# A second weight slab loaded in the retention, and a norm scale in operations of four blocks (Hyena and RetNet block, one core)

## The chip, the cores and the metric

One core of one Trainium2 chip runs the kernel. The metric is the device time of one execution in microseconds (us): the median of several executions, lowest and highest beside it. One further execution was recorded by the hardware profiler, and all rows of the trace come from that one. The engines are PE (TensorE: matrix products; its weight loads are a line of their own, PEld), DVE (VectorE), ACT (ScalarE), POOL (GpSimd, hardly used here) and SP (SyncE, which issues nearly all DMAs). Each engine takes its instructions in the order in which they stand in its queue.

## The reference

One layer works on 1024 tokens (and 256 of context) of width 1024. A norm and modulation feed one input projection; half of the columns go through a gated long convolution, half through a retention of 8 heads, in chunks of 128 tokens and in both directions; one output projection takes both halves; a second norm and an MLP with squared ReLU follow.

```python
x = x + gate1 * (concat(hyena, retention) @ w_out)
h = _modulate(_rmsnorm(x), shift2, scale2)
x = x + gate2 * (jnp.square(relu(h @ w_mlp1)) @ w_mlp2)
```

## The kernel before

**Numbers.** Each matrix product is made of three (`mm3`, lines 183 to 185): both operands are split into a high part in a shorter format and a low rest, and high x high, high x low and low x high are summed. So each operand is cast on ACT (the high part) and subtracted on DVE (the low part). Nothing is multiplied before both have been done for it.

**Weight slabs.** `slab` (from line 194) loads a slab of weights in two halves through one raw buffer (`wraw`, DMA on line 205), casts each half on ACT (206) and subtracts on DVE (207). The results go to two alternating buffers, unless the caller names a place. `prefetch()` loads the next slab in a list: the slabs of the input projection, the last four being g0, g1, q0, q1, and then o0 and o1, the first two column halves of the output weights for the convolution's part. It runs under `urgent()`, a raised priority. A scheduler sets each engine's order from priorities and dependencies; so a row in a queue need not stand where its line stands in the program.

**The entry of the retention.** The queries are computed last in the input projection: for each of two head halves `hh` and two groups, products (`pq`), a rotation on DVE (lines 569, 573, 579) and a store (1008). After each `hh` a `prefetch()` runs: o0 after the first, o1 after the second. Both take the buffers of a q slab that the products have read. Then `split_mix` reads the convolution's result, already in DRAM, in eight pieces of 128x512 through a ring of four slots (`mraw`, line 1055), and casts and subtracts each (1057, 1058) into `mx`: for k of 0 to 3 and token half 0 or 1. `out_conv(d)` multiplies all of `mx` by a 128-column block of slab o0 (d of 0 to 3) or o1 (d of 4 to 7) into `poh` (psum) and adds it to the stream XN (1069). The retention's loop over `(hh, g, j)` runs one chunk of tokens each time (`retention`; transposes `pqd`, scores `psc`, output `po`) and an `out_conv` after every second chunk. At `(0, 0, 2)` it loads slab o2, at `(1, 0, 0)` the raw data of the last slab, o3; both serve the retention's part of the output projection, at the end.

**The entry of the MLP.** `out_ret(q)` computes that part (`por`) for token half q, adds it to XN (1254), sums the squares and gives `rB2`, 1/rms of each of the 512 tokens, in all partitions. `right_factors(q, ...)` then makes the right operands of the MLP's first product. XN lies in two tiles of four 128-row blocks, XN0 and XN1. `modulated(k)` scales a block by `rB2` on DVE (1287) and applies scale and shift on ACT (1288); it runs for the blocks in the order 0, 4, 1, 5, 2, 6, 3, 7. The first product uses a scheme of seven block products in place of eight (`ORDER = (1, 5, 2, 6, 3, 7, 4)`), for which `part` (1186, 1187) splits the quarters y11, y12 (of XN0), y21, y22 (of XN1) and sums of them: b11, t1 (from y12 - y11, line 1296), b21, t2 (from u, line 1302), and b22, t3, t4. The step f=0 of the product runs for the first 256 columns, then the next 256; from f=1 on all 512 go at once.

The steps with odd f take their raw weights through CH, which has XN1's place (`w1_load`, line 1209), and WH, in XN0's place, takes the second product's weights (load 1399, sums 1401 to 1404, store 1405 to `s_d`). So both loads wait until the last part has been read from XN.

Of the kernel before, what the change touches and what calls it, by code (L numbers as in the profile page):

```python
# [12 lines left out]
AF = mybir.ActivationFunctionType  # L13
ALU = mybir.AluOpType
# [126 lines left out]
def tile_hymba_block(ctx: ExitStack, tc: tile.TileContext, I: dict, out: bass.AP, dbg=None, stop=99):  # L141
# [79 lines left out]
    def prefetch(n=1):  # L221
        for _ in range(n):
            if nxt[0] < len(order):
                key, src = order[nxt[0]]
                with urgent() if nxt[0] > 1 else ExitStack():
                    slabs[key] = slab(src, f"{key[0]}{key[1]}")
                nxt[0] += 1
# [770 lines left out]
    for hh in range(2):  # L998
        for g, ps in token_major(("q", hh), f"pq{hh}"):
            with urgent():  # L1000
                for m in range(2):
                    n0 = 4 * g + 2 * m

                    q2 = scp.tile([P, 2, 4, 2, HD], F32, tag="sc", bufs=3, name=f"q2{hh}{n0}")
                    qr = scp.tile([P, 2, 256], F32, tag="bfs", bufs=2, name=f"qr{hh}{n0}")
                    rope(qr, ps[:, 2 * m:2 * m + 2], ropes, n0, scp, f"q{hh}",
                         twice=q2.rearrange("p j h r d -> p (j h) r d"), tag="bfs", bufs=2)
                    SP.dma_start(q2_d[hh][n0:n0 + 2].rearrange("j p n -> p j n"),
                                 q2.rearrange("p j h r d -> p j (h r d)"))
            if hh == 0 and g == 0:  # L1010
                dbg("mod2", mod2)
        prefetch()
    cpool("cvp")
    cpool("vtp")
    cpool("scp")
# [122 lines left out]
    for hh in range(2):  # L1138
        for g in range(2):
            ctr = ctrs[:, g]  # L1140
            gss = rtp.tile([P, 4, 4], F32, tag="gss", bufs=2, name=f"gss{hh}{g}")
            for j in range(4):
                retention(hh, 4 * g + j, ctr, gss)
                if hh == 0 and g == 0 and j == 0:
                    for d in range(KC):
                        SP.dma_start(xn[d], I["xT"][d * P:(d + 1) * P])
                if j == 1 and pending:
                    group_norm(*pending)
                if j == 1:
                    SP.dma_start(sg.rearrange("p n d -> p (n d)"), sg_d[hh][g])  # L1150
                if j % 2:
                    out_conv(4 * hh + 2 * g + j // 2)
                if (hh, g, j) == (0, 0, 2):
                    wo = [slab(I["w_out"][2], "o2", o2)]
                if (hh, g, j) == (1, 0, 0):

                    o3r = wpool.tile([P, 4, 512], F32, tag="wh", bufs=2, name="o3r")
                    SP.dma_start(o3r, I["w_out"][3])
            pending = hh, g, sg, ctr, gss
# [116 lines left out]
    def right_factors(q, rB2, some):  # L1276
# [4 lines left out]
        def part(key, src):  # L1281
            hi, lo = B[key]
            split(hi[:, :, qs], lo[:, :, qs], src)

        def modulated(k, eng):
            y = xn[k][:, 512 * q:512 * q + 512]
            eng.tensor_tensor(y, y, rB2, op=ALU.mult)
            A.activation(y, y, AF.Identity, bias=B2[:, k:k + 1], scale=A2[:, k:k + 1])

        with urgent():  # L1290
            if 0 in some:
                for k in range(4):
                    modulated(k, V)
                    modulated(4 + k, V)
                part("b11", y11)
                V.tensor_tensor(y11, y12, y11, op=ALU.subtract)
                part("t1", y11)
                part("b21", y21)
                for h in range(2):
                    ks = slice(2 * h, 2 * h + 2)  # L1300
# [290 lines left out]
```

## Time and profile before

| | us |
|---|---|
| median of 3 runs | 1394.17 |
| lowest, highest | 1394.14, 1402.15 |
| profiled execution | 1399.48 |
| its span (first to last instruction) | 1397.7 |

The mean granted clock of TensorE in the profiled execution is 0.973 of full speed. The profiled execution lies within the three runs. Times in the rows are counted from the start of its span. In a row of the timeline the first number is the start, the second the time from there to the end of the last of a group, "x4" the number of instructions, and what stands in square brackets is how long the engine had stood idle and what ended it. Busy times of PE are modelled, and successive matmuls overlap; the distance of two starts is the price of one.

### The profile page before, as it was taken

The page shows a single profiled execution, that of the slowest core. Times are in us where ns is not written, and L with a number is a line of the kernel's source. Part 1 is how long each engine was busy: PE and PEld are TensorE (multiplying, and loading weights), DVE is VectorE, ACT ScalarE, POOL GpSimd, SP SyncE. Part 2 cuts the span into 40 slices and gives each one's busy share as a digit, 9 for nine tenths or more (in the row PEclk, how much of TensorE's full clock was granted, in tenths as well). Part 3 has the DMA queues.
Part 4 walks back from the last instruction along what each step waited for, and adds up shares of the span by engine and source line. Part 5 has one row for each costly group of instructions (what it writes and reads, how often), then busy time and mean ns, then how long its engine had stood idle before and what let it go on. Part 6 is the DMA issues. An engine that isn't in the chain of part 4 may idle for free.

```text
span 1397.7 us, 19336 instructions
## 1 busy us (share of the span) xinstructions
PE 1314.7 (94%) x7002; PEld 1108.2 (79%) x7002; DVE 974.2 (70%) x1733; ACT 533.3 (38%) x912; POOL 19.5 (1%) x24
## 2 busy tenths in 40 slices
PE   6899999999999999799996999999998999999997
PEld 1478888887788999688776788788786888888896
DVE  5889686447888775557887887887765865554563
ACT  6854422222132121223355444344444743444420
POOL 0130000000000000000000000000000000000000
PEclk9799999999999999899997999999999999999999
DMA  9445766363536644865320788899735996666621
GB/s 374 168 159 174 231 193 187 101 194 126 170 119 220 187 166 159 291 199 157 107 102 20 237 309 290 313 341 316 258 133 182 334 312 208 197 191 191 194 90 61
DMA packets 139567, 278.14 MB, mean 199 GB/s; under 512 B 14672, under 2 KB 47056, under 8 KB 137040
## 3 DMA queue, kind: packets, MB, share of 16 engines
q1 hardware_dynamic: 137744, 272.19, 58.7%
q0 software_dynamic: 1152, 4.19, 0.7%
q8 instruction: 55, 0.90, 0.3%
q10 hardware_dynamic: 576, 0.52, 0.1%
q14 instruction: 40, 0.33, 0.1%
HBM read 193.75 MB, written 83.10 MB: 198 GB/s over the span
## 4 chain that ended last, share of the span: by engine, by line
PE 70%; DVE 12%; DMA 11%; ACT 4%; issue 2%; SPq 1%; POOL 0%; DVEq 0%; ACTq 0%; POOLq 0%
PE px L183 6%; PE px L184 6%; PE px L185 6%; PE py L183 5%; PE py L184 5%; PE py L185 4%; PE pw L183 4%; PE pw L185 4%; PE pw L184 3%; DMA WH<-in_w_mlp 3%; PE pga L397 1%; DMA s_d<-WH 1%; DMA dft_f_k<-in_dft_f 1%; PE poh L183 1%; PE poh L184 1%
## 5 line engine op out<-in xcount | busy, mean ns | idle before, releaser
L1187 DVE TENSOR_TENSOR mt<-tr,mt 128x512 fp32r<-128x512 f32 x112 | 76.7, 688 | 97.0 <-ACT mt L1186 96.7
L1186 ACT CAST mt<-tr 128x512 fp32r<-128x512 f32 x112 | 69.5, 621 | 121.6 <-PE py L185 65.4
L183 PE MATMUL px<-mt,mw 128*128 128x512 f32 (+1 forms) x320 | 112.4, 352 | 2.7 <-ACT mw L1186 2.1
L184 PE MATMUL px<-mt,mw 128*128 128x512 f32 (+1 forms) x320 | 112.7, 353 | 1.2 <-DVE mt L1187 1.2
L185 PE MATMUL px<-mt,mw 128*128 128x512 f32 (+1 forms) x320 | 111.7, 350 | 0.0
L1187 DVE TENSOR_TENSOR mw<-wr,mw 128x512 fp32r<-128x512 f32 x112 | 76.6, 686 | 8.0 <-ACT mw L1186 7.5
L183 PE MATMUL py<-mt,mw 128*128 128x512 f32 x192 | 74.7, 389 | 0.0
L184 PE MATMUL py<-mt,mw 128*128 128x512 f32 x192 | 74.7, 389 | 0.0
L185 PE MATMUL py<-mt,mw 128*128 128x512 f32 x192 | 74.7, 389 | 0.0
L1186 ACT CAST mw<-wr 128x512 fp32r<-128x512 f32 x112 | 69.0, 617 | 12.2 <-DMA wr<-in_w_mlp 5.9
L183 PEld LDWEIGHTS px<-mt,mw 128*128 128x128 f32 x320 | 61.0, 191 | 11.3 <-ACT mw L1186 2.6
L184 PEld LDWEIGHTS px<-mt,mw 128*128 128x128 f32 x320 | 61.2, 191 | 9.4 <-DVE mt L1187 1.5
L185 PEld LDWEIGHTS px<-mt,mw 128*128 128x128 f32 x320 | 61.1, 191 | 8.3 <-DVE mw L1187 0.3
L183 PE MATMUL px<-hxh,wh_x 128*128 128x512 f32 x128 | 52.2, 407 | 0.0
L184 PE MATMUL px<-hxl,wh_x 128*128 128x512 f32 x128 | 51.9, 405 | 0.0
L185 PE MATMUL px<-hxh,wl_x 128*128 128x512 f32 x128 | 51.5, 402 | 0.0
L712 DVE SCALAR_TENSOR_TENSOR adac<-adaw,cs,adac 128x512 f32<-128x512 f32 x56 | 42.9, 766 | 11.7 <-DMA adaw<-in_w_ada 11.0
L185 PEld LDWEIGHTS py<-mt,mw 128*128 128x128 f32 x192 | 36.0, 188 | 7.5
L183 PEld LDWEIGHTS py<-mt,mw 128*128 128x128 f32 x192 | 36.0, 188 | 7.5
L184 PEld LDWEIGHTS py<-mt,mw 128*128 128x128 f32 x192 | 36.0, 188 | 7.4
L185 PE MATMUL pk<-wh_k,hxl 128*128 128x256 f32 x128 | 38.5, 301 | 3.3 <-DVE hxl L438 3.3
L183 PE MATMUL pk<-wh_k,hxh 128*128 128x256 f32 x128 | 40.1, 313 | 0.4 <-ACT hxh L434 0.4
(500 smaller groups left out, 3819.9 us busy)
## 6 DMA issues: line engine op xcount, KB each, us to landing
tr<-t_d SPq DMA_DIRECT2D x112, 256.0 KB, 4.0
adaw<-in_w_ada SPq DMA_DIRECT2D x64, 256.0 KB, 3.6
WH<-in_w_mlp SPq DMA_DIRECT2D x16, 1024.0 KB, 6.8
s_d<-WH SPq DMA_DIRECT2D x16, 1024.0 KB, 5.3
wr<-s_d SPq DMA_DIRECT2D x64, 256.0 KB, 4.0
wr<-in_w_mlp SPq DMA_DIRECT2D x48, 256.0 KB, 4.1
t_d<-c SPq DMA_DIRECT2D x40, 256.0 KB, 4.3
t_d<-CH SPq DMA_DIRECT2D x40, 256.0 KB, 5.0
```

Of the source, the lines that this page charges most:

```text
L183: PE.matmul(o, lhsT=lh, rhs=rh, start=first, stop=False, **kw)
L184: PE.matmul(o, lhsT=lh, rhs=rl, start=False, stop=False, **kw)
L185: PE.matmul(o, lhsT=ll, rhs=rh, start=False, stop=last, **kw)
L397: PE.matmul(pga[h][0:4, n, :], lhsT=cv[:, k, :], rhs=w_[:, n * 512:(n + 1) * 512], start=(k == 0), stop=(k == KC - 1 and i == 1))
L712: V.scalar_tensor_tensor(ac, wa, cs[:, k, 0:1], ac, op0=ALU.mult, op1=ALU.add)
L1186: A.copy(hi, src)
L1187: V.tensor_tensor(lo, src, hi.bitcast(F32), op=ALU.subtract)
```

## The change

The first part: `prefetch()` after the queries runs for `hh == 0` alone, so slab o1 is asked for inside the retention's loop, at `(0, 0, 1)`, and slab o2 one chunk later, at `(0, 0, 3)`. A debugging line that issues nothing goes. The second part: the norm scale of four blocks is one DVE operation of 128x4x512 with `rB2` repeated, followed by the four ACT operations of these blocks; blocks 0 to 3 come ahead of b11 and t1, blocks 4 to 7 behind them.

```diff
--- before.py
+++ after.py
@@ -1007,9 +1007,8 @@
                          twice=q2.rearrange("p j h r d -> p (j h) r d"), tag="bfs", bufs=2)
                     SP.dma_start(q2_d[hh][n0:n0 + 2].rearrange("j p n -> p j n"),
                                  q2.rearrange("p j h r d -> p j (h r d)"))
-            if hh == 0 and g == 0:
-                dbg("mod2", mod2)
-        prefetch()
+        if hh == 0:
+            prefetch()
     cpool("cvp")
     cpool("vtp")
     cpool("scp")
@@ -1150,7 +1149,9 @@
                     SP.dma_start(sg.rearrange("p n d -> p (n d)"), sg_d[hh][g])
                 if j % 2:
                     out_conv(4 * hh + 2 * g + j // 2)
-                if (hh, g, j) == (0, 0, 2):
+                if (hh, g, j) == (0, 0, 1):
+                    prefetch()
+                if (hh, g, j) == (0, 0, 3):
                     wo = [slab(I["w_out"][2], "o2", o2)]
                 if (hh, g, j) == (1, 0, 0):
 
@@ -1282,19 +1283,21 @@
             hi, lo = B[key]
             split(hi[:, :, qs], lo[:, :, qs], src)
 
-        def modulated(k, eng):
-            y = xn[k][:, 512 * q:512 * q + 512]
-            eng.tensor_tensor(y, y, rB2, op=ALU.mult)
-            A.activation(y, y, AF.Identity, bias=B2[:, k:k + 1], scale=A2[:, k:k + 1])
+        def modulated(i):
+
+            y = XH[i][:, :, 512 * q:512 * q + 512]
+            V.tensor_tensor(y, y, bc(rB2, 1, [P, 4, 512]), op=ALU.mult)
+            for k in range(4 * i, 4 * i + 4):
+                o = xn[k][:, 512 * q:512 * q + 512]
+                A.activation(o, o, AF.Identity, bias=B2[:, k:k + 1], scale=A2[:, k:k + 1])
 
         with urgent():
             if 0 in some:
-                for k in range(4):
-                    modulated(k, V)
-                    modulated(4 + k, V)
+                modulated(0)
                 part("b11", y11)
                 V.tensor_tensor(y11, y12, y11, op=ALU.subtract)
                 part("t1", y11)
+                modulated(1)
                 part("b21", y21)
                 for h in range(2):
                     ks = slice(2 * h, 2 * h + 2)
```

Line numbers below 1009 are the same in both; the ones behind are lower by one up to line 1150, and then higher by one (1254 becomes 1255), from the norm scale's lines on by two or three.

On SP, at the end of the queries: `wr_o11` is the raw second half of slab o1, `q214` and `q216` the last two groups of queries, `mraw` the mix ring. Before:

```order
L1036 DMA tabq_5409<-tab_d_1411 128x2048
L205 DMA wr_o11_5379<-in_w_out 128x1024
L1008 DMA q2_d1_4396<-q214_5357 128x2x512
L1055 DMA mraw_5417<-mix_d0_2896 128x512 x2
L1008 DMA q2_d1_4396<-q216_5365 128x2x512
L1055 DMA mraw_5417<-mix_d1_2897 128x512 x2
L1055 DMA mraw_5417<-mix_d2_2898 128x512 x2
L1079 DMA q2l0_0_5445<-q2_d0_4395 128x512
```

and after the change:

```order
L1035 DMA tabq_5399<-tab_d_1411 128x2048
L1054 DMA mraw_5407<-mix_d0_2896 128x512
L1008 DMA q2_d1_4396<-q214_5357 128x2x512
L1054 DMA mraw_5407<-mix_d0_2896 128x512
L1054 DMA mraw_5407<-mix_d1_2897 128x512
L205 DMA wr_o11_5552<-in_w_out 128x1024
L1008 DMA q2_d1_4396<-q216_5365 128x2x512
L1054 DMA mraw_5407<-mix_d1_2897 128x512
L1054 DMA mraw_5407<-mix_d2_2898 128x512 x2
L1054 DMA mraw_5407<-mix_d3_2899 128x512
L1078 DMA q2l0_0_5435<-q2_d0_4395 128x512
L1054 DMA mraw_5407<-mix_d3_2899 128x512
```

The second half's load stands behind three mix pieces now; the first half's, three rows above the first row shown, has not moved.

On ACT, at the same place: `wh_o1` is the high part of slab o1, `mx00` and `mx10` the high parts of the mix for the two token halves. Before:

```order
L206 CAST wh_o1_5373<-wr_o10_5375 128x1024
L206 CAST wh_o1_5373<-wr_o11_5379 128x1024
L1057 CAST mx00_5411<-mraw_5417 128x512
L1057 CAST mx10_5413<-mraw_5417 128x512
L1057 CAST mx00_5411<-mraw_5417 128x512
L1057 CAST mx10_5413<-mraw_5417 128x512
L1057 CAST mx00_5411<-mraw_5417 128x512
L1057 CAST mx10_5413<-mraw_5417 128x512
L1057 CAST mx00_5411<-mraw_5417 128x512
```

and after:

```order
L206 CAST wh_o1_5546<-wr_o10_5548 128x1024
L1056 CAST mx00_5401<-mraw_5407 128x512
L1056 CAST mx10_5403<-mraw_5407 128x512
L1056 CAST mx00_5401<-mraw_5407 128x512
L206 CAST wh_o1_5546<-wr_o11_5552 128x1024
L1056 CAST mx10_5403<-mraw_5407 128x512
L1056 CAST mx00_5401<-mraw_5407 128x512
L1056 CAST mx10_5403<-mraw_5407 128x512
L1056 CAST mx00_5401<-mraw_5407 128x512
L1056 CAST mx10_5403<-mraw_5407 128x512
```

The cast of the second half stands behind three of the eight mix casts, ahead of five. On DVE its subtraction likewise stands behind three of the eight of the mix, and that of the first half, `wl_o1`, which stood ahead of q214, stands ahead of q216. On PE 28 poh matmuls stood ahead of the one that takes the low part of the last mix piece for d = 0; 36 stand ahead of it now.

On DVE, at the MLP's entry for the second token half, from the norm scale on. The last two multiplications of eight and what follows, before:

```order
L1287 TENSOR_TENSOR XN0_5392<-XN0_5392,rB21_6804 128x512
L1287 TENSOR_TENSOR XN1_5393<-XN1_5393,rB21_6804 128x512
L1187 TENSOR_TENSOR b11l_6600<-XN0_5392,b11h_6599 128x4x256
L1187 TENSOR_TENSOR b21l_6604<-XN1_5393,b21h_6603 128x4x256
L1296 TENSOR_TENSOR XN0_5392<-XN0_5392 128x4x256
L1187 TENSOR_TENSOR b22l_6807<-XN1_5393,b22h_6806 128x4x256
L1302 TENSOR_TENSOR u210_6841<-XN1_5393,XN0_5392 128x512
L1187 TENSOR_TENSOR t1l_6602<-XN0_5392,t1h_6601 128x4x256
L1187 TENSOR_TENSOR t2l_6606<-u210_6841,t2h_6605 128x2x256
L1305 TENSOR_TENSOR XN1_5393<-XN1_5393,u210_6841 128x2x256
L1302 TENSOR_TENSOR u211_6846<-XN1_5393,XN0_5392 128x512
L1306 TENSOR_TENSOR XN0_5392<-XN1_5393,XN0_5392 128x4x256
```

and from the first multiplication on, after:

```order
L1289 TENSOR_TENSOR XN0_5382<-XN0_5382,rB21_6798 128x4x512
L1289 TENSOR_TENSOR XN1_5383<-XN1_5383,rB21_6798 128x4x512
L1188 TENSOR_TENSOR b11l_6600<-XN0_5382,b11h_6599 128x4x256
L1298 TENSOR_TENSOR XN0_5382<-XN0_5382 128x4x256
L1305 TENSOR_TENSOR u210_6829<-XN1_5383,XN0_5382 128x512
L1305 TENSOR_TENSOR u211_6834<-XN1_5383,XN0_5382 128x512
L1188 TENSOR_TENSOR b21l_6604<-XN1_5383,b21h_6603 128x4x256
L1188 TENSOR_TENSOR t1l_6602<-XN0_5382,t1h_6601 128x4x256
L1188 TENSOR_TENSOR t2l_6606<-u210_6829,t2h_6605 128x2x256
L1308 TENSOR_TENSOR XN1_5383<-XN1_5383,u210_6829 128x2x256
L1188 TENSOR_TENSOR t2l_6606<-u211_6834,t2h_6605 128x2x256
L1308 TENSOR_TENSOR XN1_5383<-XN1_5383,u211_6834 128x2x256
```

Two rows of four blocks take the place of eight, and the subtraction of b21 and that of t1 stand behind both u.

On ACT, the same place. Before, from the sixth of the eight operations on:

```order
L1288 ACTIVATE XN1_5393<-XN1_5393,mod2_1379,A2_1380 128x512
L1288 ACTIVATE XN0_5392<-XN0_5392,mod2_1379,A2_1380 128x512
L1288 ACTIVATE XN1_5393<-XN1_5393,mod2_1379,A2_1380 128x512
L1186 CAST b11h_6599<-XN0_5392 128x4x256
L1186 CAST b21h_6603<-XN1_5393 128x4x256
L1186 CAST b22h_6806<-XN1_5393 128x4x256
L1374 COPY c1_0_6996<-pw1_0_0_6997 128x256
L1186 CAST t1h_6601<-XN0_5392 128x4x256
L1357 COPY s1_1_0_256_7106<-pw1_0_256_7093 128x256
```

and after, all eight:

```order
L1377 COPY c1_0_6984<-pw1_0_0_6985 128x256
L1292 ACTIVATE XN0_5382<-XN0_5382,mod2_1379,A2_1380 128x512 x4
L1292 ACTIVATE XN1_5383<-XN1_5383,mod2_1379,A2_1380 128x512
L1187 CAST b11h_6599<-XN0_5382 128x4x256
L1292 ACTIVATE XN1_5383<-XN1_5383,mod2_1379,A2_1380 128x512 x3
L1187 CAST b21h_6603<-XN1_5383 128x4x256
L1187 CAST t1h_6601<-XN0_5382 128x4x256
L1187 CAST t2h_6605<-u210_6829 128x2x256
L1187 CAST t2h_6605<-u211_6834 128x2x256
```

The cast of b11 stands behind five of the eight operations in place of all. On SP the two loads of CH stand ahead of the first load of WH now, where a load of WH stood first, and on PE the first products of the step f=1 stand ahead of the last products (t3, t4) of f=0's second token half.

## Rows read from the trace of the kernel before

**Rows 1.** The page's first part: busy time, share of span, instructions

```profile
PE 1314.7 (94%) x7002; PEld 1108.2 (79%) x7002; DVE 974.2 (70%) x1733; ACT 533.3 (38%) x912; POOL 19.5 (1%) x24
```

**Rows 2.** Waits of PE: who waited for whom; us, times, longest one

```profile
PE poh L183 <- ACT mx L1057: 9.1, 1, 9.1
...
PE pw L183 <- ACT b11h L1186: 6.5, 1, 6.5
```

**Rows 3.** Windows: us, busy us (count) of PE, PEld, DVE, ACT, POOL; PEclk, DMA share, GB/s

```profile
566.00:579.47 13.47, 5.44 (x12) 3.66 (x13) 9.78 (x15) 3.93 (x7) 0.00 (x0) 0.62 0.77 253
...
753.94:763.70 9.76, 8.45 (x36) 7.86 (x36) 9.29 (x10) 4.05 (x6) 0.00 (x0) 0.50 0.01 2
...
763.70:773.90 10.20, 7.12 (x50) 6.07 (x49) 6.04 (x9) 5.37 (x7) 0.00 (x0) 0.99 0.51 181
...
773.90:777.40 3.50, 1.73 (x6) 1.16 (x7) 3.48 (x5) 2.45 (x5) 0.00 (x0) 1.00 0.92 306
...
777.43:780.80 3.37, 3.37 (x10) 2.61 (x8) 2.53 (x5) 1.41 (x4) 0.00 (x0) 0.51 0.88 260
...
780.80:800.00 19.20, 19.20 (x86) 15.88 (x85) 18.32 (x30) 9.06 (x15) 0.00 (x0) 1.00 0.54 199
...
940.00:980.00 40.00, 38.34 (x170) 31.45 (x169) 32.29 (x50) 17.67 (x28) 0.00 (x0) 1.00 0.91 321
```

**Rows 4.** Timeline of PE: start, us, instruction, [idle before <-releaser]

```profile
574.03 0.79 PE L183 MATMUL poh<-mx,wh_o 128*128 128x512 f32 x1 [9.06 <-ACT mx L1057]
...
574.76 0.79 PE L184 MATMUL poh<-mx,wh_o 128*128 128x512 f32 x1
...
584.97 0.40 PE L184 MATMUL poh<-mx,wh_o 128*128 128x512 f32 x1
```

**Rows 5.** Timelines of SP, ACT and DVE at the retention's entry

```profile
559.19 0.46 SPq L1036 DMA_DIRECT2D tabq<-tab_d  x1
...
565.01 1.04 ACT L206 CAST wh_o<-wr_o 128x1024 fp32r<-128x1024 f32 x1 [15.32 <-PE pq L185]
...
570.83 1.16 DVE L579 TENSOR_TENSOR q<-qr,rpq 128x1024 f32<-128x1024 f32 x1
...
571.98 1.22 DVE L207 TENSOR_TENSOR wl_o<-wr_o,wh_o 128x1024 fp32r<-128x1024 f32 x1
...
583.35 0.69 DVE L1058 TENSOR_TENSOR mx<-mraw,mx 128x512 fp32r<-128x512 f32 x1 [0.36 <-ACT mx L1057]
```

**Rows 6.** DMA issues from 566 and from 581: count, KB each, us to landing

```profile
mraw<-mix_d SPq DMA_DIRECT2D x8, 256.0 KB, 4.3
...
wr_o<-in_w_out SPq DMA_DIRECT2D x1, 512.0 KB, 3.4
...
XN<-in_xT SPq DMA_DIRECT2D x8, 512.0 KB, 7.9
```

**Rows 7.** Timelines of DVE, ACT and SP at the MLP's entry, second half

```profile
746.48 4.90 DVE L1287 TENSOR_TENSOR XN<-XN,rB 128x512 f32<-128x512 f32 x8 [0.83 <-ACT rB L1271]
...
767.67 1.21 DVE L1187 TENSOR_TENSOR t4l<-XN,t4h 128x1024 fp32r<-128x1024 f32 x1
...
747.21 5.75 ACT L1288 ACTIVATE XN<-XN,mod,A 128x512 f32<-128x512 f32 x8 [0.76 <-DVE XN L1287]
...
752.86 1.03 ACT L1186 CAST b11h<-XN 128x1024 fp32r<-128x1024 f32 x1
...
774.19 0.62 ACT L1186 CAST w<-CH 128x512 fp32r<-128x512 f32 x1
...
768.91 0.82 SPq L1209 DMA_DIRECT2D CH<-in_w_mlp  x2
```

**Rows 8.** Tile XN from 746 to 760: ns min/median/max, first and last start

```profile
L1287 DVE TENSOR_TENSOR XN<-XN,rB x8: 681/683/691, 746.5 to 750.7; 128x512 f32<-128x512 f32 x8
...
L1296 DVE TENSOR_TENSOR XN<-XN x1: 1218/1218/1218, 756.2 to 756.2; 128x1024 f32<-128x1024 f32 x1
```

**Rows 9.** Waits of DVE from 781 to 1080: us, times, longest one

```profile
DVE WH L1401 <- DMA WH<-in_w_mlp: 15.4, 10, 3.2
```


## The prediction

> **What bounds the kernel now.** I read the page first: PE is busy 94% of the span [rows 1], so only the places where PE stands still, or runs at the lower clock, can be won. The next view is PE's own waits: the long ones that the change can touch are 9.1 us ahead of poh (the first multiplication of the convolution's output), and 6.5 us ahead of pw behind b11h (the MLP's second token half) [rows 2]. The third is the windows, which give PE's busy time and clock for each stretch around these places [rows 3]. [...] Then 763.7 to 777.4 holds (10.20 - 7.12) + (3.50 - 1.73) = 4.85 us of idle PE at full clock, and 777.4 to 780.8 is low again. From 780.8 on PE has no gaps for long: 86 matmuls in 19.2 us, 0.223 us each, my price of a matmul of 512 columns at full clock. Last I read the timelines of ACT, DVE, SP and PE at both places [rows 4, 5], and the same for the MLP's entry.
>
> **Term A, the retention's entry.** Only the second half of slab o1 moves; its first half has its place still between the queries, by the order of SP. What falls away ahead of poh is one DVE subtraction (L207 at 571.98, 1.22 us) and one ACT cast of 1.04 us; the mix loads, which stood on SP behind that half's DMA and its wait for a free buffer, now come right behind tabq's load at 559.19 [rows 5]. A mix load lands in 4.3 us [rows 6], so the first piece is there when ACT is free: cast of the first half until 565.01 + 1.04 = 566.05, cast of mix 0.62, first poh at 566.7 instead of 574.03. It is one or two matmuls only, since the next needs the low part, which stands on DVE behind the last query operation. That one ends at 571.98 as before (the first half's subtraction has moved from ahead of the one query to ahead of the other, and the sum is the same), and 0.69 us later, at 572.7, PE can go on; before, the same matmul began at 574.76 [rows 4].
>
> How much of these 2.1 us stays is decided by the last of the eight mix pieces, since the ring has four slots. The second half's load is issued when DVE has freed its buffer, which is right ahead of the last query operation at 570.83 [rows 5], lands 3.4 us later [rows 6] at 574.3 to 574.9, and takes 1.04 us on ACT and 1.22 on DVE ahead of the fourth mix piece, whose slot the eighth waits for: 577.9, plus 4.3 of landing, 0.62 and 0.69, is 583.5; before, that subtraction ended at 584.04 [rows 5]. So the last pieces come hardly sooner, and PE gains by having done more ahead of them. Of PE's order I take the matmul with the low part of poh0's last piece (584.97, [rows 4]): 28 poh matmuls stand ahead of it before, 36 now. It begins some 0.2 us sooner with 8 x 0.223 = 1.8 us more done: A = -2.0. Bounds: -4.9, if PE also came to its full clock earlier (2.1, and 12 matmuls at 5.44 / 12 = 0.45 instead of 0.223, [rows 3]); +4.1, if the loads of the second half and of the eighth piece land like those of XN a little later, in 7.9 instead of 3.4 and 4.3 [rows 6] (583.5 + 4.5 + 3.6 = 591.6, less 0.7 that PE was slack, against 584.97, less the 1.8). I take -2.0: the mix loads' own landing is the nearest row.
>
> **Term B, the entry of the MLP.** Eight DVE multiplications of 512 elements, alternating over both XN, become two of 2048; ACT's eight operations stay, but four for XN0 come first and b11h's cast after the fifth. A DVE operation of 2048 elements is not in the trace. 512 take 0.68 and 1024 take 1.22 [rows 8], so 0.54 for each further 512: 0.68 + 3 x 0.537 = 2.29 us as an estimate. The eight take 4.90 us in a row [rows 7], the two 4.5. Bounds: 2.0 (a quarter of the row of eight less the fixed part of three) and 2.7 (four single ones). In the second half, which PE waits for, b11h's cast begins 2.29 + 0.04 + 5 x 0.72 = 5.93 us after DVE's start (ACT's eight take 5.75, [rows 7]) instead of 752.86 - 746.48 = 6.38: -0.45.
>
> [...]
>
> The first token half's operations run beside por matmuls of the second half; that DVE is done 0.4 us sooner there I count at nothing, since those matmuls hide it.
>
> Behind that, t1 moves: its low part stands behind u and b21l now, and is there some 1.7 us after PE wants it, in place of waits of about 1.1: +0.6. All four parts of b22, t3 and t4 come nevertheless earlier, since DVE has less to do and t4 comes ahead of t3: t4l's last read of XN1 ends near 765.2 instead of 767.67 + 1.21 = 768.88 [rows 7]. On this hangs more than the part: the raw weights of step f=1 lie in XN1's place, and their load (768.91, and first on SP now, ahead of the w2 load) goes 3.7 us earlier; ACT's first cast of them, 774.19, comes to some 770.5. That is the end of the idle time from 763.7 to 777.4: of its 4.85 us 2.0 stay, -2.85; and of the low clock in 777.4 to 780.8, which follows that wait and costs 3.37 x 0.5 = 1.7, I count 1.2 as gone. B = -0.45 + 0.6 - 2.85 - 1.2 = -3.9. Bounds: -7.4 (all 4.85 and 1.7, and the cast's 0.45 with twice as much again hidden in the row, 0.4 more) and +5.6 (step f=1's first products stand on PE now ahead of the 24 last matmuls of f=0's second token half; where f=1's weights are not earlier, these 24 wait behind them, and cost 8.45 / 36 = 0.235 each at the low clock, [rows 3]).
>
> **Nothing else.** Slab o2 is loaded one chunk later; its first use lies in retention's end, tens of us later, and PE is without a gap meanwhile: at nothing, and at most 1 us if ACT's queue stands for its raw data. The line that goes (a debug hook) issues nothing. From the MLP's middle PE's order is the same.
>
> **Sum.** -2.0 - 3.9 = -5.9 us; 1399.48 of the profiled execution become 1393.6. That execution lay 5.3 above the median of the runs shown; a difference carries over: 1394.17 - 5.9 = 1388.3.
>
> **Rivals.** (1) The gain is given back in the first MLP product: there DMA is busy 0.91 of the time [rows 3], and DVE waits ten times, 15.4 us, for the w2 loads [rows 9]. If these set the pace, only what the loads gain counts. Their chain starts behind the same release, 3.7 earlier, so up to 2.5 of the 5.9 goes: -3.4, 1390.8. Against it: PE has no gap from 780.8 to 800, and stands still for 1.7 of the 40 us from 940 alone.
>
> (2) The second half of o1 comes late into ACT's queue and holds the five mix casts behind it, and the XN loads crowd its load: A = +4.1 in place of -2.0, sum +0.2, 1394.4. For it: these XN loads need 7.9. Against it: they are issued after it.
>
> (3) Slower. PE's clock stays low longer: waits that were one long piece (then ten us of full clock from 763.7) become several short ones, b11, t1l, u, and then f=1's weights, so that 763.7 to 773.9 also runs at 0.5. Its 50 matmuls would take 8.45 / 36 - 7.12 / 50 = 0.093 us more each, 4.7 us, and the next 24 of 512 columns 0.45 - 0.22 = 0.23 more, 5.5: -5.9 + 10.2 = +4.3, 1398.5. It decides from where more than 5.9 us of full-clock work fall to the low level. For it: four stretches of 0.50 to 0.62 stand right behind waits [rows 3]; against it: 763.7 to 773.9 ran at 0.99 with PE idle for 3 of 10 us.
>
> [...]
>
> That the change does not do what it says is part of A: half of the slab still stands beside the queries.
>
> **Chances.** Forecast 0.55 (own range 1383 to 1391), given back 0.25, late slab 0.10, low clock 0.10. From 1383 (near both lower bounds: -12.3 would be 1381.9) to 1398 (about case 3) more than eight in ten lie. A measurement of this kernel tells about 1% (13.9 us) from no change; none of the cases reaches that, so 0.03 on either side and 0.94 for the same.
>
> **What would show it.** Right: poh's first matmuls near 567 and steady from 572.7, PE's wait ahead of it 2 us in place of 9.1 but a second one near 6 behind it; two L-lines of four blocks with about 2.3 us each; f=1's loads some 3.7 us earlier against the wait ahead of b11h; no low stretch after 777. Wrong: the eighth mix piece later than 584; w2 waits grown by the gain; 763 to 774 at a clock of 0.5.

## The result, and the profile after

The changed kernel takes 1380.53 us (median of 4 runs, 1379.25 to 1382.74) against 1394.16 us of the kernel before beside it (4 runs, 1393.37 to 1402.15): a ratio of 0.9891, 95% interval 0.9852 to 0.9930. With more runs (below) it was 0.9914, 0.9884 to 0.9945, which is about 12 us. The forecast was 1388.3 us, with 1383 to 1398 as its range: right in the direction, too small by half, and the time lies outside the range. The profiled execution of the changed kernel took 1379.41 us, its span 1377.6.

Those two profiled executions lie 20.1 us apart, more than the medians. The first rows to look at are the last matmul of the queries and the first of `por`; between the two lies the whole retention. Timeline of PE, the last matmul of the queries before:

```profile
564.69 0.28 PE L185 MATMUL pq<-wh_q,hxl 128*128 128x256 f32 x1
```

and from the same matmul on in the kernel after (the last row is the first matmul from which PE goes on):

```profile
556.84 0.28 PE L185 MATMUL pq<-wh_q,hxl 128*128 128x256 f32 x1
...
558.77 0.50 PE L183 MATMUL poh<-mx,wh_o 128*128 128x512 f32 x1 [1.66 <-ACT mx L1056]
...
564.79 0.79 PE L184 MATMUL poh<-mx,wh_o 128*128 128x512 f32 x1 [2.30 <-DVE mx L1057]
```

The queries end at 556.84 in place of 564.69, 7.9 us earlier, though PE's matmuls up to there are the same, in the same order. This part of the kernel scatters from run to run (a second execution of before, below, shows it), so a difference of two executions has to be taken between fixed points behind it. The first `por` matmul, kernel before:

```profile
662.20 0.40 PE L183 MATMUL por<-mr,o2h 128*128 128x512 f32 x1
```

and kernel after:

```profile
652.45 0.40 PE L183 MATMUL por<-mr,o2h 128*128 128x512 f32 x1
```

From the last query matmul to the first `por`: 662.20 - 564.69 = 97.5 us before, 652.45 - 556.84 = 95.6 after. Behind it PE's order differs between kernels, so I count work: the time from the first `por` matmul until PE has done 900 x 256 columns of matmuls (some way into the step f=1), whatever their order. Windows of just this length, kernel before (148.60 us), and in it the stretches 56 to 61 and 73.5 to 78.5 us behind the first `por`; columns as in [rows 3]:

```profile
662.20:810.80 148.60, 128.98 (x647) 107.67 (x646) 123.18 (x205) 69.12 (x115) 0.00 (x0) 0.92 0.38 123
718.20:723.20 5.00, 5.00 (x15) 3.97 (x16) 4.97 (x6) 2.91 (x5) 0.00 (x0) 0.66 0.56 211
735.70:740.70 5.00, 4.80 (x26) 4.68 (x27) 5.00 (x6) 1.15 (x3) 0.00 (x0) 0.66 0.27 105
```

and kernel after (140.02 us):

```profile
652.45:792.47 140.02, 123.14 (x648) 103.16 (x646) 121.63 (x192) 68.57 (x115) 0.00 (x0) 0.95 0.38 130
708.45:713.45 5.00, 5.00 (x24) 4.12 (x23) 4.86 (x7) 5.00 (x8) 0.00 (x0) 1.00 0.56 213
725.95:730.95 5.00, 4.64 (x37) 4.44 (x38) 4.37 (x11) 0.20 (x1) 0.00 (x0) 1.00 0.03 11
```

The same work takes 8.6 us less. Two things make it up: PE stands still for 148.60 - 128.98 = 19.6 us before and 140.02 - 123.14 = 16.9 after; and the clock is full in both short stretches where it was 0.66. Summed over slices of half a microsecond, as busy time times what the clock lacks, the low clock costs 9.4 us before and 3.6 after; the rest is 119.6 and 119.5, PE's own work at full clock, and it is nearly the same in every run below (118.9 to 120.1). So 2.7 us come from idle time and 5.8 from the clock.

PE's waits after, answering to [rows 2]:

```profile
PE pw L183 <- ACT b11h L1187: 6.0, 1, 6.0
...
PE poh L183 <- DVE rpq L573: 2.7, 1, 2.7
...
PE poh L184 <- DVE mx L1057: 2.3, 1, 2.3
...
PE por L183 <- DVE XN L1255: 2.2, 2, 1.7
```

The 9.1 us ahead of poh have become 1.7, 2.7 and 2.3, and b11's 6.5 are 6.0. The windows from the second half's b11 on, answering to [rows 3]:

```profile
740.66:750.03 9.37, 7.03 (x28) 6.15 (x28) 9.20 (x11) 6.72 (x11) 0.00 (x0) 0.50 0.00 0
750.03:757.01 6.98, 5.40 (x39) 4.79 (x39) 4.69 (x7) 2.99 (x5) 0.00 (x0) 0.99 0.47 156
757.01:763.36 6.35, 6.35 (x34) 5.30 (x33) 6.10 (x11) 5.35 (x9) 0.00 (x0) 1.00 1.01 368
920.00:960.00 40.00, 40.00 (x178) 32.91 (x176) 32.89 (x52) 16.45 (x27) 0.00 (x0) 1.00 0.90 320
```

The low clock behind b11 is still there (0.50), but from 750 on PE runs at full clock and from 757 without a gap, where [rows 3] had 4.85 us of idle time and then 0.51. Timelines of DVE, ACT, SP and PE at that place, answering to [rows 7]:

```profile
733.71 4.49 DVE L1289 TENSOR_TENSOR XN<-XN,rB 128x2048 f32<-128x2048 f32 x2 [0.83 <-ACT rB L1272]
...
751.41 1.22 DVE L1188 TENSOR_TENSOR t4l<-XN,t4h 128x1024 fp32r<-128x1024 f32 x1
...
739.58 1.03 ACT L1187 CAST b11h<-XN 128x1024 fp32r<-128x1024 f32 x1
...
756.16 0.62 ACT L1187 CAST w<-CH 128x512 fp32r<-128x512 f32 x1
...
752.66 0.82 SPq L1210 DMA_DIRECT2D CH<-in_w_mlp  x2
...
746.87 0.58 PE L184 MATMUL py<-t1l,w 128*128 128x256 f32 x1 [1.48 <-DVE t1l L1188]
```

The two four-block operations take 4.49 us; t4l ends at 752.63, the load of CH is issued at 752.66, 12.0 us behind b11's first matmul at 740.66 where it was 768.91 - 753.94 = 15.0; the first cast of f=1's weights is 15.5 behind it where it was 20.25. So 3.0 of those 4.75 us are an earlier issue and 1.7 an earlier landing, as the DMA rows show (issues, KB each, us to landing). Before, from 767 on:

```profile
WH<-in_w_mlp SPq DMA_DIRECT2D x2, 1024.0 KB, 7.1
CH<-in_w_mlp SPq DMA_DIRECT2D x2, 512.0 KB, 5.4
```

After, from 752 on:

```profile
WH<-in_w_mlp SPq DMA_DIRECT2D x2, 1024.0 KB, 8.2
CH<-in_w_mlp SPq DMA_DIRECT2D x2, 512.0 KB, 3.8
```

Behind that nothing is given back: from the first `por` to the first matmul of the second MLP product it is 408.0 and 405.8 us in two executions of before, and 396.9, 398.5 and 395.9 in three with the new norm scale.

### The profile page after: what moved, and what is told of

It reads as the page before. It is cut to its first block, busy times and chain, and to the rows that moved or that the text cites. A ratio compares the mean times of both kernels' runs of the same rounds, so it can differ in the third digit from the quotient of the medians.

```text
span 1377.6 us, 19333 instructions
## 1 busy us (share of the span) xinstructions
PE 1303.4 (95%) x7002; PEld 1099.6 (80%) x7002; DVE 974.3 (71%) x1721; ACT 532.9 (39%) x912; POOL 19.5 (1%) x24
## 4 chain that ended last, share of the span: by engine, by line
PE 77%; DVE 10%; DMA 6%; ACT 4%; issue 2%; POOL 0%; SPq 0%; DVEq 0%; ACTq 0%; POOLq 0%
PE px L183 6%; PE px L185 6%; PE px L184 6%; PE py L183 5%; PE py L185 5%; PE py L184 5%; PE pw L183 5%; PE pw L185 5%; PE pw L184 5%; PE pga L397 1%; PE pGv L900 1%; PE pq L185 1%; PE pq L184 1%; PE pq L183 1%; PE po L1104 1%
## 5 line engine op out<-in xcount | busy, mean ns | idle before, releaser
L1188 DVE TENSOR_TENSOR mt<-tr,mt 128x512 fp32r<-128x512 f32 x112 | 76.8, 688 | 97.8 <-ACT mt L1187 97.5
```

The source lines that it names most:

```text
L1188: V.tensor_tensor(lo, src, hi.bitcast(F32), op=ALU.subtract)
```

## The experiments

All runs in one table. "Work done" is the time from the first `por` to 900 x 256 columns, "idle" and "low clock" its two losses, all in us of the one profiled execution; the ratio is that of the timed runs to before, with its interval. I read the causes from the three columns of the profile; single executions of before lay between 1384.7 and 1402.4 us, so the ratios of small edits overlap.

| run | work done | idle | low clock | ratio (95%) |
|---|---|---|---|---|
| before | 148.6 | 19.6 | 9.4 | |
| before again | 148.3 | 19.6 | 9.0 | |
| slab alone | 147.2 | 19.7 | 7.5 | 0.9991 (0.9964 to 1.0017) |
| norm scale alone | 140.0 | 16.7 | 4.1 | 0.9946 (0.9919 to 0.9972) |
| the change | 140.0 | 16.9 | 3.6 | 0.9891 (0.9852 to 0.9930) |
| the change again | 140.0 | 16.7 | 3.7 | 0.9914 (0.9884 to 0.9945) |
| four blocks, old order | 150.7 | 23.4 | 7.8 | 0.9978 (0.9951 to 1.0004) |
| single blocks, new order | 144.0 | 16.3 | 8.5 | 0.9956 (0.9934 to 0.9979) |
| the same, w1 first | 143.6 | 16.1 | 8.6 | 0.9950 (0.9922 to 0.9977) |
| old norm scale, w1 first | 144.1 | 18.1 | 6.1 | 0.9966 (0.9936 to 0.9995) |
| first token half alone | 145.8 | 20.3 | 5.4 | 0.9975 (0.9954 to 0.9996) |
| second token half alone | 141.8 | 16.8 | 5.8 | 0.9924 (0.9897 to 0.9950) |
| one DVE operation more | 143.3 | 17.4 | 7.0 | 0.9935 (0.9908 to 0.9961) |
| quarters | 142.0 | 15.1 | 7.5 | 0.9942 (0.9913 to 0.9971) |
| quarters in the second half | 140.8 | 15.9 | 5.4 | 0.9931 (0.9910 to 0.9951) |
| the same, w1 first | 140.6 | 14.7 | 6.6 | 0.9923 (0.9893 to 0.9952) |

### The two parts apart, and both kernels again

The slab alone is the diff's first two pieces on the kernel before:

```diff
-        prefetch()
+        if hh == 0:
+            prefetch()
...
-                if (hh, g, j) == (0, 0, 2):
+                if (hh, g, j) == (0, 0, 1):
+                    prefetch()
+                if (hh, g, j) == (0, 0, 3):
```

> The slab part alone (norm scale as before). Theory S (the gain is made in the two stretches that the change touches, and the 8 us by which the profiled executions differ ahead of the first poh matmul are their own scatter): -2.0 us against before, read in the profile as 2 us between the last pq matmul and the chunk loop's steady poh work, and the MLP's entry as before, with 6.5 us ahead of b11 and the low clock behind 777. Rival E (something of the change also reaches the code ahead of it, by the way that buffers or loads come to lie): -4 us or more, with PE ahead of the first poh matmul some us faster than in before.

The norm scale alone is the third:

```diff
-                for k in range(4):
-                    modulated(k, V)
-                    modulated(4 + k, V)
+                modulated(0)
                 part("b11", y11)
...
+                modulated(1)
                 part("b21", y21)
```

> The norm scale alone (slab o1 beside the queries as before). Theory S: -9.6 us against before: 2.6 of it by the end of the first token half's products, 6.4 from there to the first products of the step f=1, 0.6 behind; the 9 us wait ahead of poh stays. Rival P (my prediction's sizes): -3.9. Rival E: -11 or more, with the part ahead of the retention faster.

> The changed kernel once more, nothing edited. Theory S: -11.7 us (the sum of the two parts), with the start of the first poh matmul anywhere within some us. Rival E: -13.6 as measured first, and PE ahead of poh again some 8 us faster than in a second execution of before.

> The kernel before once more, nothing edited, for a second profile. Theory S: ahead of the last pq matmul this execution differs from the first profile of before by several us, though the code is the same, and from there on it keeps the same distances. Rival E: the last pq matmul at 564.7 within 1 us, as in the first profile.

The last query matmul of the second execution of before (timeline of PE):

```profile
558.18 0.28 PE L185 MATMUL pq<-wh_q,hxl 128*128 128x256 f32 x1
```

558.18 where it was 564.69: 6.5 us of scatter in the same instructions, so rival E falls. In the 16 executions this matmul lies between 553.9 and 567.2. The slab alone, its last query matmul and its first `por`:

```profile
557.52 0.28 PE L185 MATMUL pq<-wh_q,hxl 128*128 128x256 f32 x1
...
653.61 0.39 PE L183 MATMUL por<-mr,o2h 128*128 128x512 f32 x1
```

96.1 us between them. With the old slab the stretch took 97.5, 98.5 and 98.1, with the new one 95.0 to 96.1 in thirteen executions: 2.5 us, shown in the trace. The timed ratio alone (-1.3 us, between -5.0 and +2.4) could not have told it from nothing. The norm scale alone has all of the change's gain in work done (140.0), and its timed gain is 7.5 us, between 3.9 and 11.3. The sum, 2.5 + 8.4 = 10.9, is what the repeated runs of the change give (11.0 between the medians); the timed gains of the two parts come to 8.8, with intervals wide enough for both. The rest of the 13.6 and of the 20.1 between the first pair is scatter.

### Width or order

All runs from here on have the slab moved as in the change. Four-block operations on DVE, all else in the old order (set against the kernel before; `modulated(i)` is now the multiplication of four blocks alone, `shifted(k)` the ACT operation of one block):

```diff
-                for k in range(4):
-                    modulated(k, V)
-                    modulated(4 + k, V)
+                modulated(0)
+                modulated(1)
+                for k in range(4):
+                    shifted(k)
+                    shifted(4 + k)
```

> The slab moved, the norm scale as two operations of four blocks on DVE, but all eight ACT operations ahead of b11, as before, and the w2 load again first on SP. The stretch from the second token half's first product b11 to the step f=1's product b21 takes 29.0 us in before and 22.7 in the change. Theory O (the gain of 6.3 us there comes from the order: parts that need XN0 alone run ahead of the other blocks, XN1 is let go first, and f=1's weights are loaded ahead of the w2 load): 28.5 here, only some 0.5 less than before, and b11 waits longer than 6.3 us. Rival W (the width: fewer and longer DVE operations, so all of DVE's chain comes sooner): 24 or less.

Single-block operations in the new order (against the change):

```diff
         def modulated(i):
 
-            y = XH[i][:, :, 512 * q:512 * q + 512]
-            V.tensor_tensor(y, y, bc(rB2, 1, [P, 4, 512]), op=ALU.mult)
             for k in range(4 * i, 4 * i + 4):
                 o = xn[k][:, 512 * q:512 * q + 512]
+                V.tensor_tensor(o, o, rB2, op=ALU.mult)
```

> The slab moved, the norm scale in the change's order (blocks 0 to 3, b11, t1, blocks 4 to 7, b21) but as eight DVE operations of one block; in this build t3 stays ahead of t4 and the w2 load first on SP. Theory O: in the stretch of 29.0 before and 22.7 after, some 26, since the part of the order that lets XN1 go first is missing. Rival W: 28.5 or more. The wait ahead of b11 by either: about 6.1 us, as ACT is ready for b11 after five operations, and 0.5 us of it hangs on ACT alone.

Timeline of PE with four blocks in the old order: `por`'s wait in the first half, b11's in the second, and the first product of f=1:

```profile
713.58 0.50 PE L183 MATMUL por<-mr,o3h 128*128 128x512 f32 x1 [1.71 <-DVE XN L1255]
...
751.51 0.58 PE L183 MATMUL pw<-b11h,w 128*128 128x256 f32 x1 [8.52 <-ACT b11h L1187]
...
773.81 0.50 PE L183 MATMUL pw<-b11h,w 128*128 128x512 f32 x1 [2.29 <-ACT w L1187]
```

Width by itself loses: 3.5 us against the slab alone. ACT has all eight operations ahead of b11, which waits 8.5 us in place of 6.5, and f=1's weights come late by 2.3 us of waiting. Rival W falls. Yet the first row is worth keeping: `por`'s wait is 1.71 us, and behind it the clock stays full (1.00, 56 to 61 us behind the first `por`). Single blocks in the new order gain 3.2 us against the slab alone, by idle time (16.3 for 19.7), while the low clock grows:

```profile
712.81 0.80 PE L183 MATMUL por<-mr,o3h 128*128 128x512 f32 x1 [3.30 <-DVE XN L1255]
...
755.41 0.39 PE L184 MATMUL py<-b22l,w 128*128 128x256 f32 x1 [2.15 <-DVE b22l L1188]
```

Here `por` waits for 3.3 us, with low clock behind it (0.52, 56 to 61 us behind the first `por`), and b22's low part for 2.2. The wait ahead of b11 that I expected at 6.1 is not there: products of the first half (t4) stand right ahead of it on PE, and PE waits 4.28 us in front of those. So neither width nor order has the gain alone.

The expectations go by the stretch from the second half's b11 to f=1's b21. It is 29.8 us with four blocks in the old order and 24.9 with single blocks in the new one, as theory O had it in direction. But PE's order differs between these kernels, so the stretch does not hold the same products in each; so I go by the work done.

### The order of two loads

In the change, the raw weights of f=1 stand ahead of the w2 load on SP. To force that elsewhere, the first two w2 loads wait for f=1's weights, by a DVE operation that reads a column of CH and writes one of WH:

```diff
         r = WH[:, 4 * (f % 2):4 * (f % 2) + 4]
+        if f < 2:
+            g = CH[:, 2, 0:1]
+            with urgent():
+                V.tensor_tensor(r[:, 0, 0:1], g, g, op=ALU.subtract)
```

> The slab moved, the norm scale wholly as before, and the first two w2 loads wait until f=1's first raw weights have landed. Theory O: the stretch of 29.0 falls to about 27 (1.8 us of earlier landing), by the load's order alone; the wait of 6.8 us ahead of b11 stays. Rival B: 29. If it falls to 24 or less, the order of the two loads alone is the cause of the gain in this stretch.

> As the run with eight DVE operations in the new order, and the first two w2 loads wait, by one DVE operation of a column each, until f=1's first raw weights have landed: so these stand first on SP and have the DMA engines for themselves. Theory O: the stretch falls to about 24, 2 us less than without this, by an earlier landing of f=1's weights (3.4 us after issue in place of 5.2). Rival B (what is gained is not the load's but PE's or ACT's chain in front of f=1's first product): no change against the run without it.

The stretches behind 20 us after the second half's b11 (3.5 and 3.4 us), with the slab alone:

```profile
763.98:767.48 3.50, 1.80 (x7) 1.17 (x8) 3.50 (x6) 2.46 (x5) 0.00 (x0) 0.99 0.80 270
767.48:770.88 3.40, 3.40 (x10) 2.64 (x9) 2.49 (x5) 1.38 (x4) 0.00 (x0) 0.51 0.91 289
```

and with the w1 load first, the norm scale old as well:

```profile
768.07:771.57 3.50, 3.30 (x17) 2.33 (x15) 2.76 (x5) 2.62 (x6) 0.00 (x0) 1.00 0.86 279
771.57:774.97 3.40, 3.40 (x15) 2.79 (x16) 3.40 (x7) 2.29 (x5) 0.00 (x0) 1.00 0.71 267
```

PE is busy 3.3 of 3.5 us in place of 1.8, and the low clock behind it is gone. That is 3.1 us of work done (147.2 to 144.1) by the order of two loads, more than the 2 I expected, because the clock came with it: 1.6 of idle time and 1.4 of low clock. A few of f=1's first products moved ahead on PE with it, so by the stretch of the expectation, 29.1 to 23.4 us, it looks like nearly all of the gain, and by work done it is 3.1 of the change's 7.2. In the single-block kernel it gave 0.4 of work done and 1.5 of the stretch (24.9 to 23.4); there only 0.25 us of waiting for f=1's weights had been left.

### A token half at a time, and a wait made longer

The new norm scale in one token half, the old one in the other (here the new one in the first; the other run has `q == 1` in both places; `modulated4` is the change's function, `modulated` that of before):

```diff
-                modulated(0)
+                if q == 0:
+                    modulated4(0)
+                else:
+                    for k in range(4):
+                        modulated(k, V)
+                        modulated(4 + k, V)
...
-                modulated(1)
+                if q == 0:
+                    modulated4(1)
```

> The slab moved; the change's norm scale in the first token half alone, the second half as before. Measure: the time from the first por matmul until PE has done the same amount of columns behind it (900 x 256 of them); 148.6 and 148.3 in two executions of before, 147.2 with the slab alone, 140.0 in three of the change. Idle PE and low clock make up all differences there. Theory C (the low clock is the larger part of the gain: three stretches of it, each of 3.5 us, are gone): por's wait is 1.75 us, and the stretch of low clock behind it goes, so that 145 here; the 29 us from b11 of the second half on stay. Rival I (idle time alone counts, and the clock is chance): 147, with 0.4 less idle.

> The slab moved; the change's norm scale in the second token half alone, the first half as before. By the same measure as the run on the first half alone: theory C: por's wait is 2.13 us again and the low clock behind it comes back; from b11 of the second half on as in the change; 142 to 143.5. Rival I: 140.5.

First half new: `por`'s wait, and the first product of f=1 at the end, where the second half is old:

```profile
709.59 0.50 PE L183 MATMUL por<-mr,o3h 128*128 128x512 f32 x1 [1.75 <-DVE XN L1255]
...
764.71 0.50 PE L183 MATMUL pw<-b11h,w 128*128 128x512 f32 x1 [2.47 <-ACT w L1187]
```

Second half new, the first old:

```profile
710.83 0.76 PE L183 MATMUL por<-mr,o3h 128*128 128x512 f32 x1 [2.12 <-DVE XN L1255]
```

145.8 and 141.8: theory C's numbers, within 0.8 and 0.3 us. `por`'s wait in the two kernels themselves, before:

```profile
718.12 0.50 PE L183 MATMUL por<-mr,o3h 128*128 128x512 f32 x1 [2.13 <-DVE XN L1254]
```

and after:

```profile
707.96 0.50 PE L183 MATMUL por<-mr,o3h 128*128 128x512 f32 x1 [1.75 <-DVE XN L1255]
```

What `por` waits for are four additions to XN, which read what it multiplied before and stand behind the norm scale on DVE. Timeline of DVE, before and after:

```profile
716.66 2.72 DVE L1254 SCALAR_TENSOR_TENSOR XN<-por,mod,XN 128x512 f32<-128x512 f32 x4
...
706.51 2.72 DVE L1255 SCALAR_TENSOR_TENSOR XN<-por,mod,XN 128x512 f32<-128x512 f32 x4
```

PE goes on 1.46 and 1.45 us behind their start, so what shortens the norm scale shortens the wait (4.91 to 4.49 us on DVE, 2.13 to 1.75 on PE). The test of the cause adds one DVE operation to the change, ahead of the first half's norm scale, and leaves PE's order as it is:

```diff
+                if q == 0:
+                    pad = B["t1"][1][:, 0:3, 256:384]
+                    V.tensor_tensor(pad, bc(rB2[:, 0:128], 1, [P, 3, 128]), bc(rB2[:, 0:128], 1, [P, 3, 128]), op=ALU.mult)
                 modulated(0)
```

> The changed kernel with one more DVE operation of 128x384 (about 0.47 us), whose result nobody reads, ahead of the norm scale of the first token half alone; PE's order is the same. Theory C: por's wait ahead of its next matmul grows from 1.75 to 2.2 us, and with it the stretch of low clock behind it comes back, about 1.7 us lost: 140.0 becomes 142 or more, four times what the operation takes. Rival I: 140.5.

```profile
710.20 0.50 PE L183 MATMUL por<-mr,o3h 128*128 128x512 f32 x1 [2.22 <-DVE XN L1255]
...
727.63 0.38 PE L183 MATMUL pw<-t2h,w 128*128 128x256 f32 x1 [1.77 <-ACT s L1363]
```

The operation takes 0.56 us, `por`'s wait grows from 1.75 to 2.22, and the stretches that the change had at full clock are low again, windows as above:

```profile
710.22:715.22 5.00, 5.00 (x15) 4.00 (x16) 4.86 (x7) 5.00 (x8) 0.00 (x0) 0.66 0.56 211
727.72:732.72 5.00, 4.75 (x27) 4.46 (x28) 4.94 (x6) 1.56 (x4) 0.00 (x0) 0.66 0.27 105
```

Work done goes from 140.0 to 143.3: 3.3 us for an operation of 0.56. Idle time gives 0.5 of it and the low clock 3.4 (3.6 to 7.0); the rest is 0.6 less. Of the low clock 1.7 us lie right behind `por`'s wait and 1.6 in the second stretch, where the wait for t2h has grown too (0.67 in the change, 1.77 here). Over all sixteen executions: where `por`'s wait was 1.71 to 1.75 us (seven of them) the clock behind it stayed full (1.00 in the stretch 56 to 61 us behind the first `por`); where it was 2.12 to 3.30 (nine) it fell to 0.5 for 3.2 us and more (0.52 to 0.68 in that stretch), at least 1.6 us lost each time. So rival I falls for the clock behind this wait; the second stretch is another matter (below, what stays open). The lengths hold for this place alone: with four blocks in the old order a wait of 1.94 us ahead of the first half's b11 has full clock behind it, while before the change two waits of 0.98 and 0.81 us, 1.5 us apart, have the low clock of f=1's first products (0.51, [rows 3]) behind them.

### Towards a better version

The norm scale in quarters, so that b11 waits for one quarter (the second argument of `modulated` is the half of the 512 tokens):

```diff
-                modulated(0)
+                modulated(0, 0)
                 part("b11", y11)
+                modulated(0, 1)
...
-                modulated(1)
+                modulated(1, 0)
                 part("b21", y21)
+                modulated(1, 1)
```

> The changed kernel with the norm scale in quarters (four blocks of 256 tokens, DVE operations of 128x4x256 and ACT operations of 256), in the order in which the products need them, so that b11 waits for one quarter alone. Theory C: the wait ahead of the second half's b11 falls from 6.0 to about 4 us, the low clock behind it stays: 138 by the same measure, 2 us below the change. Rival A (ACT's sixteen shorter operations cost as much as they save, each with its fixed part): 140 or more, with t1, b21 and b22 late.

```profile
706.45 0.80 PE L183 MATMUL por<-mr,o3h 128*128 128x512 f32 x1 [2.98 <-DVE XN L1255]
...
737.32 0.58 PE L183 MATMUL pw<-b11h,w 128*128 128x256 f32 x1 [3.89 <-ACT b11h L1187]
...
750.28 0.38 PE L184 MATMUL py<-b22l,w 128*128 128x256 f32 x1 [1.74 <-DVE b22l L1188]
```

The wait ahead of b11 falls to 3.9 as expected, but `por`'s rises to 3.0 with low clock behind it (0.66, 56 to 61 us behind the first `por`), b22 waits 1.7, and work done is 142.0: rival A's number, with a wait of `por` that it had not named. So the quarters were put into the second half alone, without and with the w1 load first:

```diff
-                modulated(0)
-                part("b11", y11)
+                if q:
+                    modulated(0, 0, 256)
+                    part("b11", y11)
+                    modulated(0, 256, 512)
+                else:
+                    modulated(0)
+                    part("b11", y11)
```

> The changed kernel, and in the second token half alone XN0's four blocks are scaled in two operations of 128x4x256 in place of one, so that b11 waits for a quarter; in this build t3 stands ahead of t4 and the w2 load first on SP again. By the measure of 900 x 256 columns behind the first por matmul (140.0 in the change). Theory C: the first half stays free of low clock (por's wait 1.75); the wait ahead of b11 falls from 6.0 to about 4, but f=1's weights come late again with idle PE and a stretch of low clock behind them: 141.5 to 143. Rival A: 138, the 2 us less of waiting kept.

> As the run with the quarters in the second half alone, and the first two w2 loads wait until f=1's first raw weights have landed. Theory C: without the late weights 138.5, below the change's 140.0, and in time about 1.5 us below the changed kernel. If it is not at least 2 us below the run without this wait, the order of the two loads is not what decides there.

Both lie at the change's level (140.8 and 140.6; the second has a stretch of low clock 11 us behind the first `por` that no other run has, and is 0.9 us late from there on). The first was expected at 141.5 to 143, with f=1's weights late and low clock behind them; neither is there, so that reason was wrong. Idle time falls to 14.7 in the second, but the low clock takes it back: 6.6 for 3.6. The two differ by 0.2 us, 1.1 without that delay, and not the 2 that I had set as the mark, so with this chain the order of the loads does not decide. No version beat the change.

## Why the prediction was wrong, by its steps

- **Term A held.** Behind the last query matmul the forecast had the first poh after 2.0 us, steady work after 8.0, the last mix subtraction done after 18.8. Measured: 558.77 - 556.84 = 1.9, 564.79 - 556.84 = 8.0, and 575.82 - 556.84 = 19.0. Timelines of SP, ACT and DVE after: the second half's load, its cast, and the last mix subtraction.

```profile
563.03 0.33 SPq L205 DMA_DIRECT2D wr_o<-in_w_out  x1
...
568.35 1.05 ACT L206 CAST wh_o<-wr_o 128x1024 fp32r<-128x1024 f32 x1 [2.91 <-DMA wr_o<-in_w_out]
...
575.13 0.69 DVE L1057 TENSOR_TENSOR mx<-mraw,mx 128x512 fp32r<-128x512 f32 x1
```

  The load landed in 5.3 us, between the 3.4 taken and the 7.9 of the rival, and its cast came 1.3 to 1.9 us later than forecast; the fourth to seventh mix pieces followed without a gap. -2.0 was forecast, -2.5 measured. Rival 2 did not happen.
- **The operations held.** 2.29 us was the estimate for one of 2048 elements, 4.49 us the measured pair; the wait ahead of b11 fell by 0.52, forecast 0.45. (The bound of 2.0 us that the prediction gives for one operation is half of the row of eight, not a quarter, less three fixed parts of 0.15 us, by 2 x 0.683 - 1.218 of [rows 8].) Six such parts would have made the row 0.9 us shorter, as an estimate; 4.90 - 4.49 = 0.4 was measured. The 0.4 more that the lower bound of B counts as hidden in the row is shown by no run; ahead of b11 the wait fell from 6.54 to 6.02, 0.52 in all.
- **Idle time in the MLP's entry held in sum.** -0.45 + 0.6 - 2.85 = -2.7 was forecast, 19.6 - 16.9 = -2.7 measured. That is in part luck, for two misses cancelled: t1 cost 1.0 more, not 0.6 (waits of 0.18 and 1.48 for 0.63), and f=1's weights came 4.75 us sooner, not 3.7, since the shorter landing ahead of the w2 load had not been counted.
- **The step that failed is the price of the clock, in two sentences.** "I count 1.2 as gone" took one stretch of low clock, the one from 777; that stretch went, all 1.7 of it. And "that DVE is done 0.4 us sooner there I count at nothing, since those matmuls hide it" was wrong: por waits for DVE there (2.13 us before, 1.75 after), and the 0.4 us decided whether the clock fell behind it. In place of -1.2 the clock gave -5.8 (9.4 to 3.6): 1.7 at `por`, 1.7 in the stretch 74 to 78 us behind the first `por`, 1.7 at f=1's first products, the rest behind b11. So the mechanism of the other terms was right, and the clock was mis-sized by 4.6 us, which is nearly all by which B failed (-3.9 forecast, -8.6 measured). That the time lies below the range owes something to scatter too: 1394.17 - 10.9 would be 1383.3, and beside the later runs the kernel before had medians of 1391.4 to 1392.2.
- **Rival 1 (given back) did not happen:** PE has no gap in 40 us of the DMA-fed stretch, at a DMA share of 0.90, and DVE's waits there for the w2 loads are 8.8 us in place of 15.4 [rows 9]. **Rival 3 (slower by the clock)** had the mechanism, with the wrong sign for this change: shorter waits gave clock back (9.4 us of loss became 3.6; it counts four low stretches behind waits; [rows 3] has three). That it can go the other way is shown by the one operation more, where the low clock grows from 3.6 to 7.0. The four-block operations in the old order lose by idle time instead (23.4 for 19.7; low clock 7.8 for 7.5).
- **What stays open:** the stretch of low clock 74 to 78 us behind the first `por` is there in both executions of before and with the longer wait, and is missing with the slab alone and in five other runs that have the low clock behind por's wait. The two waits ahead of it are 1.25 and 0.49 us in before, and 1.24 and 0.49 in three of those runs, the slab alone among them: their length does not decide it. What brings it on was not found. So of the 5.8 us 1.7 may be luck of before, and the slab alone may owe its 1.3 us behind the first `por` to that. Against the slab alone, which lacks this stretch too, the change gives 7.2 us: 2.8 of idle time and 3.9 of low clock. Each edited kernel but the change also has a single profile.

## What to carry to other kernels

Put a price on the clock for every wait of PE that an edit shortens or lengthens, the ones of two microseconds too: here 0.5 us of wait more brought 1.7 us of low clock right behind it, and cost 3.3 us in all. When runs scatter by more than the edit, compare the time for the same amount of PE work between two fixed points of the trace, and split it into idle time, low clock and the rest; the rest should come out equal (here 118.9 to 120.1 us). And look at which of two loads that wait for the same release is issued first: here the one whose data PE needs next, put first, gave 3.1 us of work done with the old norm scale, and 0.4 with single blocks.

## What the runs showed of the hardware that was not expected

- The clock behind one wait of PE: at its full level (1.00) after 1.71 to 1.75 us in seven executions, at 0.5 for 3.2 us and more of the stretch 56 to 61 us behind the first `por` after 2.12 to 3.30 us in nine.
- The part of the kernel up to the last query matmul, with PE's matmuls the same in all sixteen executions, took between 553.9 and 567.2 us, so that one profile against another says little about 10 us in 1390.
- Two loads of 512 KB landed in 3.8 us in the change, issued ahead of two of 1024 KB, and in 5.4 before, issued 1.5 us behind one.
